# A spectral filter stage in a fused attention and long-convolution kernel: a ring block's matrix products issued one step after its VectorE work, and a mix with the projections by weights

## The chip, the cores and the metric

The kernel runs on one core of a Trainium2 chip. The core has five engines with a queue of instructions each: TensorE (PE, matmuls; PEld is its weight load), VectorE (DVE), ScalarE (ACT), GpSimd (POOL) and SyncE (SP, which here only issues DMAs). Each engine works its own list in order; semaphores hold an instruction back until what it reads is there or the buffer it writes is free. The metric is the device time of the whole program in microseconds (us), and less is better. The kernel before takes 1736.26 us, the median of three runs from 1733.69 to 1740.81.

## The reference, cut to what matters

Two layers of a backbone run over 1024 latent tokens and 256 context tokens of width 1024: a latent attention layer and a gated long convolution. The long convolution multiplies spectra, and the spectra of its filters depend on parameters alone, so the kernel can compute them at any time before layer 1. This is the part that the change touches:

```python
def hyena_filter_spectra(L, w_in, w_hid, b, freq, w_out):
    ...
    for k, w in enumerate((w_in, w_hid[0], w_hid[1])):
        hdn = jnp.sin(freq[k] * (hdn @ w.astype(f32) + b[k]))
    h = (hdn @ w_out.astype(f32)).reshape(L, HY_ORDER, 2, HY_WIDTH)
    ...
    h = h * jnp.exp(-t * deltas)[:, None, None, :]
    hf, hb = h[:, :, 0], h[:, :, 1]
    k_circ = jnp.concatenate([hf[:1] + hb[:1], hf[1:], jnp.zeros_like(hf[:1]), hb[:0:-1]], axis=0)
    return jnp.fft.rfft(k_circ, axis=0)
```

Beside it runs the input projection of layer 0, `t @ w_in` in `mla_mixer`, which gives the queries' and keys' latent vectors, the rotary key and the gate.

## The kernel before, in words

All matrix products run in a reduced precision format, on operands split in two: `split` (L95) makes a high part on ScalarE (`copy`, L96) and a low part on VectorE (subtract, L97), and `mm3` (L117) multiplies three of the four pairs (L119, L120, L121). So every operand that a matmul reads has passed through ScalarE and VectorE.

`layer0_in` (L462) runs three kinds of work together:

- **The filter stage**, the generator `filters` (L286). After a small network (`filter_mlp`) it goes through eight groups of 128 channels. For each group g there are eight position blocks j: a decay tile `dec` of 128 KB is loaded (L314, two buffers), four matmuls make `ph` (L318, L319, two banks), VectorE multiplies it by `dec` into `kk` (L321) and forms the sum `kp` and the difference `km` (L328, L329). Then `ring` (L222, L225, VectorE alone) folds the group's eight blocks into eight blocks `blk` of a transform. Each block goes through `forward`: its split into `bh` (ScalarE) and `bl` (VectorE), then the products with the transform's matrices `fm` into a bank `u` (9 matmuls, 12 for block 0, so 75 of them for a group). ScalarE copies `u` to `ko` (L340), and SyncE stores it to `kd` (L351).
- **The projections**, the generator `work`, 46 steps: gate tiles, the latent keys with their norms, the rotary key, the context stream. Its matmuls write the banks `pj` and read the tiles `pg` (activations, split once) and `w` (weights, loaded into `wr` and split as they are needed, three buffers). A step is mostly 12 such matmuls. After `work` comes `latent_q`, three tiles of queries with their norms and two more gate tiles.
- **The modulation vectors**, the generator `ada`: weights `aw` are loaded in 512 KB pieces and multiplied by one column into the bank `ad` (L128).

A yield of these generators is where the next one may put its instructions. In the kernel before, `filters` yields once for each j and once after each ring block, 128 times; nine of these are used up before the mixing loop, and the loop then takes one step of `work` for every two steps of `filters` (L621). The projections' 46 steps are so given out after some 92 of the 119 steps that are left.

The place in the program is not the order on the engines. A list scheduler takes the program's order as priority and writes a fixed list for each engine, taking a later instruction first where it reckons that the earlier one is not ready. The lists, not the yields, are what the chip runs. Below, *group g* is one of the eight channel groups, numbered from 0, *its first u* is the first matmul that writes `u` for it, and *round g* is the stretch from the first u of group g-1 to that of group g. *The last ring product* is the last matmul on `u` of group 7. What stands behind it up to the first attention score (`apx`) is called *the tail*.

Of the kernel before, what the change touches and what calls it, by code (L numbers as in the profile page):

```python
# [24 lines left out]
KD = D // P  # L25
# [30 lines left out]
class Net:  # L56
# [227 lines left out]
    def filters(self, psum, pt_h, pt_u, side):  # L284
# [15 lines left out]
        def load(g):  # L300
            wr = rp.tile([P, 512], F32, tag="fwr", name="fwr", bufs=1)
            wh, wl = [rp.tile([P, 512], F32R, tag=f"fw{r}", name="fw", bufs=1) for r in range(2)]
            nc.sync.dma_start(out=wr, in_=a["fwout"][g])
            self.split(wr, wh, wl)
            return wh, wl

        nxt = load(0)
        for g in range(KD):
            wh, wl = nxt
            kp = [gp.tile([P, 4, CS], F32, tag="rg", name=f"kp{i}") for i in range(2)]  # L310
            km = [gp.tile([P, 4, CS], F32, tag="rg", name=f"km{i}") for i in range(2)]
            for j in range(8):
                dec = rp.tile([P, 2, 1, P], F32, tag="dec", name="dec", bufs=2)
                nc.sync.dma_start(out=dec, in_=a["dec"][g, j])  # L314
                ps = psum.tile([P, 2, 2, P], F32, tag=pt_h, name="ph")
                ts = slice(P * j, P * j + P)
                for d, h in ((0, self.hf), (1, self.hr)):
                    nc.tensor.matmul(ps[:, d], lhsT=h[:, ts], rhs=wh[:, 256 * d : 256 * d + 256], start=True, stop=False)  # L318
                    nc.tensor.matmul(ps[:, d], lhsT=h[:, ts], rhs=wl[:, 256 * d : 256 * d + 256], start=False, stop=True)  # L319
                kk = rp.tile([P, 2, 2, P], F32, tag="kk", name="kk")  # L320
                nc.vector.tensor_tensor(out=kk, in0=ps, in1=dec.broadcast_to([P, 2, 2, P]), op=ALU.mult)  # L321
                if j == 0:
                    bias = rp.tile([1, 2, P], F32, tag="hb", name="hbias", bufs=1)
                    nc.sync.dma_start(out=bias, in_=a["hbias"][:, :, P * g : P * g + P])
                    nc.vector.tensor_tensor(out=kk[0:1, 0], in0=kk[0:1, 0], in1=bias, op=ALU.add)
                k0 = kp[j // 4][:, j % 4].rearrange("p (o c) -> p o c", o=2)
                k1 = km[j // 4][:, j % 4].rearrange("p (o c) -> p o c", o=2)
                nc.vector.tensor_tensor(out=k0, in0=kk[:, 0], in1=kk[:, 1], op=ALU.add)  # L328
                nc.vector.tensor_tensor(out=k1, in0=kk[:, 0], in1=kk[:, 1], op=ALU.subtract)  # L329
                if j == 0:  # L330
                    nc.vector.tensor_copy(out=km[0][0:1, 0], in_=kp[0][0:1, 0])
                yield
            if g + 1 < KD:
                nxt = load(g + 1)
            cl = slice((g % 2) * P, (g % 2) * P + P)

            def emit(i, b):
                u = self.forward(two, ubank, fm, i, b)
                ko = rp.tile([P, 2, CS], F32, tag="ko", name="ko")
                nc.scalar.activation(out=ko, in_=u, func=AF.Copy, scale=1.0 / 1024)  # L340
                r0 = 2 * i + 1
                if i == 0:
                    r0 = 0
                    kx = rp.tile([P, CS], F32, tag="kx", name="kx", bufs=1)
                    nc.vector.tensor_scalar(out=ko[0:1], in0=ko[0:1], scalar1=0.5, scalar2=None, op0=ALU.mult)
                    nc.scalar.copy(out=kx, in_=ko[:, 0])
                    nc.scalar.copy(out=kx[0:1], in_=ko[0:1, 1])
                    nc.vector.memset(ko[0:1, 1], 0.0)
                for o in range(2):
                    oc = slice(P * o, P * o + P)  # L350
                    nc.sync.dma_start(out=self.kd[o, g // 2, :, r0 : r0 + 2, cl], in_=ko[:, :, oc])  # L351
                    if i == 0:
                        nc.sync.dma_start(out=self.kd[o, g // 2, :, 2, cl], in_=kx[:, oc])

            for i, b in self.ring(two, lambda: gp.tile([P, 1024], F32, tag="rg", name="rg"), kp, km, False):
                emit(i, b)
                yield
        self.close("filtg", "filtr", "filt")


# [94 lines left out]
    def layer0_in(self):  # L455
# [16 lines left out]
        filt = self.filters(ps, "ph", "pu", "right")  # L472
# [144 lines left out]
                pass  # L617

        todo = work()
        n = 0  # L620
        for step, _ in enumerate(filt):  # L621
            while n * 120 < (step + 1) * 60:
                next(todo, None)
                n += 1
        for _ in todo:
# [822 lines left out]
```

## Time and profile before

| what | value |
| --- | --- |
| time, median of three runs | 1736.26 us |
| the profiled execution, its own time | 1731.71 us |
| span of its instructions | 1729.9 us |
| TensorE busy | 1633.5 us, 94% |
| VectorE busy | 1442.2 us, 83% |
| ScalarE busy | 766.3 us, 44% |
| mean granted TensorE clock | 0.979 |
| first `kk` and last `kk` of the filter stage | 26.9 and 376.4 us |
| first and last matmul on `u` of the stage | 59.8 and 403.3 us |
| first attention score (`apx`) | 439.8 us |

The profile takes one execution, 4.55 us shorter than the median of the three runs. "Busy" is the union of an engine's instructions; matmuls are pipelined and their modelled ends overlap the next one's start, so the start-to-start distance of matmuls in a dense run is the time that one takes, and not its listed duration. A wait is put down to the instruction or transfer that came last. Line numbers are those of the kernel before; the same functions stand up to ten lines further down after the change.

### The profile page before, as it was taken

Reading aid. Unit: us, or ns where it says so; the run is one execution under the profiler, and the core shown is the slowest. Engines: PE = TensorE matmul, PEld = TensorE weight load, DVE = VectorE, ACT = ScalarE, POOL = GpSimd, SP = SyncE. Lnnn points to the kernel's source line nnn. Section 1 sums busy time; section 2 is a strip of 40 time slices with the busy share of each in tenths; the row PEclk is TensorE's granted clock in tenths of the full one; section 3 lists DMA queues with packets and bytes.
Section 4 is the critical chain, followed back from the end, with each engine's and each line's share of the span. In section 5 each row is a group of like instructions: output and inputs, shape, how many; then the busy total and the mean of one; then the engine's idle time right before and its main releaser. Section 6 shows DMA issues by size and latency. Waiting matters only on the chain.

```text
span 1729.9 us, 22940 instructions
## 1 busy us (share of the span) xinstructions
PE 1633.5 (94%) x8160; PEld 1299.5 (75%) x8160; DVE 1442.2 (83%) x2558; ACT 766.3 (44%) x1337; POOL 16.0 (1%) x43
## 2 busy tenths in 40 slices
PE   5899897899999999999999999999999999999996
PEld 2467676787788788788787777888888888887874
DVE  4886979895699899899899456999999999999856
ACT  4533444445455465555555345433433433343313
POOL 1000000000000000000000010000000000000000
PEclk9899999899999999999999999999999999999998
DMA  9777664436101001010014771332332332244545
GB/s 342 256 231 222 200 187 120 138 89 206 28 27 37 25 32 38 19 33 25 25 56 132 232 254 64 101 98 83 101 115 83 104 106 89 95 122 134 180 142 197
DMA packets 140759, 206.15 MB, mean 119 GB/s; under 512 B 13578, under 2 KB 71649, under 8 KB 140516
## 3 DMA queue, kind: packets, MB, share of 16 engines
q1 hardware_dynamic: 137508, 194.00, 35.7%
q0 software_dynamic: 3136, 10.69, 1.9%
q8 instruction: 64, 1.05, 0.3%
q14 instruction: 51, 0.42, 0.1%
HBM read 148.92 MB, written 53.61 MB: 117 GB/s over the span
## 4 chain that ended last, share of the span: by engine, by line
PE 75%; DVE 10%; DMA 9%; ACT 3%; issue 2%; SPq 1%; DVEq 0%; ACTq 0%
PE pj L121 12%; PE pj L119 12%; PE pj L120 12%; DMA dec<-in_dec 2%; PE O L120 2%; PE S L119 2%; PE O L119 2%; PE S L826 2%; PE O L121 2%; PE apx L762 2%; PE S L825 2%; PE S L121 2%; PE S L120 2%; PE apx L763 2%; PE fu L119 2%; PE fy L119 2%
## 5 line engine op out<-in xcount | busy, mean ns | idle before, releaser
L96 ACT CAST w<-wr 128x512 fp32r<-128x512 f32 (+1 forms) x149 | 90.7, 609 | 259.5 <-PE pj L120 129.5
L119 PE MATMUL pj<-a,w 128*128 128x512 f32 x512 | 203.1, 397 | 1.7 <-ACT a L422 1.6
L121 PE MATMUL pj<-a,w 128*128 128x512 f32 x512 | 203.1, 398 | 0.0
L120 PE MATMUL pj<-a,w 128*128 128x512 f32 x512 | 203.0, 397 | 0.0
L828 ACT ACTIVATE p<-S 128x512 f32<-128x512 f32 x160 | 95.7, 598 | 148.2 <-DVE acc L835 69.5
L97 DVE TENSOR_TENSOR w<-wr,w 128x512 fp32r<-128x512 f32 (+1 forms) x149 | 98.8, 671 | 54.7 <-ACT w L96 54.6
L96 ACT CAST bh<-raw 128x512 fp32r<-128x512 f32 x128 | 77.1, 620 | 89.1 <-DVE raw L1071 71.0
L119 PEld LDWEIGHTS pj<-a,w 128*128 128x128 f32 x512 | 96.4, 188 | 22.0 <-ACT a L422 2.4
L120 PEld LDWEIGHTS pj<-a,w 128*128 128x128 f32 x512 | 96.5, 188 | 19.9 <-DVE a L423 0.2
L121 PEld LDWEIGHTS pj<-a,w 128*128 128x128 f32 x512 | 96.6, 189 | 19.5 <-issue 0.8
L97 DVE TENSOR_TENSOR p<-p 128x512 fp32r<-128x512 f32 x160 | 109.4, 684 | 1.5 <-ACT p L96 1.2
L764 DVE TENSOR_REDUCE cm<-apx 128x1 f32<-128x512 f32 (+1 forms) x192 | 107.1, 591 | 3.8 <-PE apx L763 3.1
L835 DVE TENSOR_TENSOR acc<-acc,p 128x512 f32<-128x512 f32 x144 | 98.7, 685 | 7.6 <-ACT p L828 6.7
L121 PE MATMUL pj<-pg,w 128*128 128x512 f32 (+1 forms) x248 | 96.5, 389 | 8.7 <-DVE w L97 8.6
L96 ACT CAST p<-p 128x512 fp32r<-128x512 f32 x160 | 99.5, 622 | 4.8
L119 PE MATMUL pj<-pg,w 128*128 128x512 f32 (+1 forms) x248 | 95.7, 389 | 2.7 <-ACT pg L422 2.7
L120 PE MATMUL pj<-pg,w 128*128 128x512 f32 (+1 forms) x248 | 96.6, 389 | 0.6 <-DVE pg L423 0.6
L97 DVE TENSOR_TENSOR bl<-raw,bh 128x512 fp32r<-128x512 f32 x128 | 84.7, 686 | 9.1 <-ACT bh L96 9.0
L119 PE MATMUL u<-bh,fm 128*128 128x256 f32 (+1 forms) x200 | 68.2, 342 | 12.2 <-ACT bh L96 9.5
L762 PE MATMUL apx<-kn,qn 128*128 128x512 f32 (+1 forms) x192 | 69.0, 364 | 2.2 <-DVE cm L764 1.9
L321 DVE TENSOR_TENSOR kk<-ph,dec 128x512 f32<-128x512 f32 x64 | 42.6, 684 | 33.2 <-DMA dec<-in_dec 26.6
L763 PE MATMUL apx<-krh,r 128*128 128x512 f32 (+1 forms) x192 | 67.1, 357 | 0.0
(312 smaller groups left out, 4408.9 us busy)
## 6 DMA issues: line engine op xcount, KB each, us to landing
aw<-in_adaw SPq DMA_DIRECT2D x32, 512.0 KB
kd<-ko SPq DMA_DIRECT2D x128, 128.0 KB
wr<-in_hw SPq DMA_DIRECT2D x64, 256.0 KB
kt<-kd SPq DMA_DIRECT2D x56, 256.0 KB
wr<-in_w SPq DMA_DIRECT2D x34, 256.0 KB
dec<-in_dec SPq DMA_DIRECT2D x64, 128.0 KB
pg<-in_adaw SPq DMA_DIRECT2D x32, 256.0 KB
wr<-in_wo SPq DMA_DIRECT2D x32, 256.0 KB
```

The source lines that it names most:

```text
L96: self.nc.scalar.copy(out=hi, in_=raw)
L97: self.nc.vector.tensor_tensor(out=lo, in0=raw, in1=hi, op=ALU.subtract)
L119: mm(out, lhsT=w[0], rhs=x[0], start=start, stop=False)
L120: mm(out, lhsT=w[0], rhs=x[1], start=False, stop=False)
L121: self.last = mm(out, lhsT=w[1], rhs=x[0], start=False, stop=stop)
L321: nc.vector.tensor_tensor(out=kk, in0=ps, in1=dec.broadcast_to([P, 2, 2, P]), op=ALU.mult)
L762: mm(b[:, :w], lhsT=qn[0][:, c], rhs=kn[0][:, o : o + w], start=True, stop=False)
L763: mm(b[:, :w], lhsT=r1[:, c], rhs=krh[:, o : o + w], start=False, stop=True)
L764: v.tensor_reduce(out=cm[:, t, i : i + 1], in_=b[:, :w], axis=AX.X, op=ALU.max)
L825: mm(S, lhsT=krh[:, c], rhs=r1, start=False, stop=False)
L828: act.activation(out=p, in_=S, func=AF.Exp, scale=ASCALE)
L835: v.tensor_tensor(out=acc, in0=acc, in1=p, op=ALU.add)
```

## The change

The step of `filters` now yields a weight: 3 for a position block j, 5 for each of three empty steps between the first ring block's VectorE work and anything else, and 4 for each ring block's products. The products of a block (with its split, its `ko` and its stores) are issued when the next block's ring work has been issued, and those of the last block at the end. A group weighs 3 x 8 + 5 x 3 + 4 x 8 = 71. The mixing loop gives out one step of `work` for every 8 x 67 / 50 = 10.72 of weight.

```diff
@@ -329,7 +329,7 @@
                 nc.vector.tensor_tensor(out=k1, in0=kk[:, 0], in1=kk[:, 1], op=ALU.subtract)
                 if j == 0:
                     nc.vector.tensor_copy(out=km[0][0:1, 0], in_=kp[0][0:1, 0])
-                yield
+                yield 3
             if g + 1 < KD:
                 nxt = load(g + 1)
             cl = slice((g % 2) * P, (g % 2) * P + P)
@@ -352,9 +352,17 @@
                     if i == 0:
                         nc.sync.dma_start(out=self.kd[o, g // 2, :, 2, cl], in_=kx[:, oc])
 
+            held = None
             for i, b in self.ring(two, lambda: gp.tile([P, 1024], F32, tag="rg", name="rg"), kp, km, False):
-                emit(i, b)
-                yield
+                if held is None:
+                    for _ in range(3):
+                        yield 5
+                else:
+                    emit(*held)
+                    yield 4
+                held = i, b
+            emit(*held)
+            yield 4
         self.close("filtg", "filtr", "filt")
 
 
@@ -617,9 +625,10 @@
                 pass
 
         todo = work()
-        n = 0
-        for step, _ in enumerate(filt):
-            while n * 120 < (step + 1) * 60:
+        n = passed = 0
+        for weight in filt:
+            passed += weight or 0
+            while n * KD * 67 < passed * 50:
                 next(todo, None)
                 n += 1
         for _ in todo:
```

No instruction is added or removed. What the lists of the engines make of it is seen at three places. In the rows, `ph` is the filter's product, `u` a ring product, `pj<-pg,w` a projection, `ad` and the `pj` with `ident`, `rms` or `st` are short pieces of the modulation and the norms.

**First, TensorE ahead of the first u of group 3.** Before, the row that starts group 4's `ph` is followed by a piece of a norm and 61 projection matmuls in a row, of which the first are shown:

```order
L319 MATMUL ph<-fw,hr 128x256
L318 MATMUL ph<-fw,hf 128x256
L414 MATMUL pj<-ident,rms 128x128 x4
L119 MATMUL pj<-pg,w 128x512
L120 MATMUL pj<-pg,w 128x512
L121 MATMUL pj<-pg,w 128x512
L119 MATMUL pj<-pg,w 128x512
```

Now the last `ph` of group 3, a piece of a norm, two blocks of group 4's `ph` and two steps of the modulation are all that stands there, and group 3's first u follows:

```order
L318 MATMUL ph<-fw,hr 128x256
L319 MATMUL ph<-fw,hr 128x256
L404 MATMUL pj<-ident,st 128x64 x4
L318 MATMUL ph<-fw,hf 128x256
L319 MATMUL ph<-fw,hf 128x256
L318 MATMUL ph<-fw,hr 128x256
L319 MATMUL ph<-fw,hr 128x256
L318 MATMUL ph<-fw,hf 128x256
L319 MATMUL ph<-fw,hf 128x256
L318 MATMUL ph<-fw,hr 128x256
L319 MATMUL ph<-fw,hr 128x256
L128 MATMUL ad<-aw,sc 32x512 x8
```

Round 3 held 61 projection matmuls and now holds 2.

**Second, VectorE at the first blocks of group 4.** Before, four instructions make two blocks, then come a piece of the context's modulation, the low parts of both blocks, and the next two blocks:

```order
L222 SCALAR_TENSOR_TENSOR rg<-rg 128x512 x2
L222 SCALAR_TENSOR_TENSOR blk<-rg 128x256 x4
L423 SCALAR_TENSOR_TENSOR pg<-pg,adac_87 128x256
L97 TENSOR_TENSOR bl<-blk,bh 128x512 x2
L222 SCALAR_TENSOR_TENSOR blk<-rg 128x256 x4
```

Now the order of the ring's own instructions is the same, with a piece of the later blocks' work where the modulation stood:

```order
L222 SCALAR_TENSOR_TENSOR rg<-rg 128x512 x2
L222 SCALAR_TENSOR_TENSOR blk<-rg 128x256 x4
L225 TENSOR_TENSOR rt<-rg 128x256
L97 TENSOR_TENSOR bl<-blk,bh 128x512 x2
L222 SCALAR_TENSOR_TENSOR blk<-rg 128x256 x4
```

Two blocks stand ahead of the first low part in both.

**Third, TensorE at the end of the stage.** Before, the last ring product is followed by the norm of the query tiles, after 647 + 13 of the 744 projection matmuls; 84 of them stand behind it:

```order
L121 MATMUL u<-bh,fm_104 128x256
L414 MATMUL pj<-ident,rms 128x128 x4
L128 MATMUL pj<-st,ones 32x512 x3
L119 MATMUL pj<-pg,w 128x512
L120 MATMUL pj<-pg,w 128x512
L121 MATMUL pj<-pg,w 128x512
L119 MATMUL pj<-pg,w 128x512
L396 MATMUL pj<-ident,st 128x96 x4
```

Now it is followed by 76 projection matmuls before those norms come, and 172 stand behind it:

```order
L119 MATMUL u<-bh,fm_103 128x256
L120 MATMUL u<-bl,fm_103 128x256
L121 MATMUL u<-bh,fm_104 128x256
L121 MATMUL pj<-pg,w 128x512
L119 MATMUL pj<-pg,w 128x512
L120 MATMUL pj<-pg,w 128x512
L121 MATMUL pj<-pg,w 128x512
L119 MATMUL pj<-pg,w 128x512
```

So 88 projection matmuls have moved from ahead of the last ring product to behind it.

## The prediction

> **What bounds the kernel now.** I read the page first, then the stretch of the filter stage cut at the first u of each group, then the waits of that stretch. The page gives the two engines that matter, and in its slices the stage lies in the first ten:
>
> ```profile
> span 1729.9 us, 22940 instructions
> PE 1633.5 (94%) x8160; PEld 1299.5 (75%) x8160; DVE 1442.2 (83%) x2558; ACT 766.3 (44%) x1337; POOL 16.0 (1%) x43
> PE   5899897899999999999999999999999999999996
> DVE  4886979895699899899899456999999999999856
> ```
>
> Over the whole span TensorE is the bound, so the end moves by what TensorE loses. It loses in slices 1 to 10, where VectorE is as full as it is. The cut by rounds (length; busy of PE, PEld, DVE, ACT, POOL; clock; DMA) shows which engine sets the pace of each; rows 1 to 7 are rounds 1 to 7, the eighth the ring products of group 7, the ninth the tail:
>
> ```profile
> 59.80:128.10 68.30, 62.39 (x337) 41.68 (x338) 56.82 (x119) 34.30 (x63) 0.00 (x0) 0.96 0.70 221
> 128.10:178.40 50.30, 47.95 (x264) 36.86 (x262) 33.32 (x70) 17.71 (x32) 0.00 (x0) 1.00 0.66 193
> 178.40:221.40 43.00, 36.96 (x199) 28.80 (x198) 39.03 (x88) 19.45 (x36) 0.00 (x0) 0.92 0.66 202
> 221.40:265.80 44.40, 39.75 (x222) 31.67 (x220) 35.02 (x74) 18.21 (x31) 0.00 (x0) 0.97 0.61 187
> 265.80:308.60 42.80, 29.53 (x183) 25.30 (x183) 39.36 (x83) 19.07 (x38) 0.00 (x0) 0.90 0.42 122
> 308.60:352.90 44.30, 43.85 (x217) 36.60 (x218) 36.07 (x81) 19.83 (x35) 0.00 (x0) 0.93 0.44 128
> 352.90:387.30 34.40, 34.01 (x185) 28.93 (x184) 31.23 (x64) 14.16 (x27) 0.00 (x0) 1.00 0.38 112
> 387.30:403.60 16.30, 16.30 (x100) 13.48 (x101) 12.73 (x29) 12.48 (x23) 0.00 (x0) 1.00 0.45 128
> 403.60:439.80 36.20, 32.24 (x145) 25.03 (x143) 14.62 (x28) 14.66 (x26) 3.70 (x7) 0.95 0.70 209
> ```
>
> Rounds 1, 2, 4, 6 and 7 are TensorE's. Rounds 3 and 5 are VectorE's: it is idle for 43.00 - 39.03 = 4.0 and 42.80 - 39.36 = 3.4 us, and TensorE waits. The longest of these waits is this one:
>
> ```profile
> 308.64 0.80 PE L119 MATMUL u<-bh,fm 128*128 128x512 f32 x1 [7.46 <-ACT bh L96]
> ```
>
> It is round 5's end. A group's first u must wait for its whole ring: in round 7, where no other work of VectorE lies between, the last two `kk` start at 375.84 and the first u at 387.26, so some 11 us after the group's last `ph` are VectorE's alone, and TensorE needs as much other work on its list there.
>
> ```profile
> 375.84 1.29 DVE L321 TENSOR_TENSOR kk<-ph,dec 128x512 f32<-128x512 f32 x2 [1.20 <-DMA dec<-in_dec]
> 387.26 0.49 PE L119 MATMUL u<-bh,fm 128*128 128x512 f32 x1 [0.39 <-ACT bh L96]
> ```
>
> **What TensorE's list is worth.** In dense stretches matmuls start this far apart:
>
> ```profile
> 318.09 0.28 PE L120 MATMUL u<-bl,fm 128*128 128x256 f32 x1
> 319.29 0.28 PE L121 MATMUL u<-bh,fm 128*128 128x256 f32 x1
> 322.14 0.39 PE L119 MATMUL pj<-pg,w 128*128 128x512 f32 x1
> 323.95 0.39 PE L121 MATMUL pj<-pg,w 128*128 128x512 f32 x1
> 115.48 1.07 PE L128 MATMUL ad<-aw,sc 128*32 128x512 f32 x8
> 319.71 0.38 PE L414 MATMUL pj<-ident,rms 128*128 128x128 f32 x2
> ```
>
> The first pair is 10 matmuls apart, 0.12 us each at 256 columns; the second 8 apart, 0.226 us each at 512. A modulation step takes about 1.0 us, a small transpose 0.15. Counting every matmul of each round in the lists at these prices gives, for rounds 1 to 7, the last ring products and the tail, in us:
>
> - before: 56.5, 45.8, 32.9, 37.8, 24.0, 39.5, 33.1, 15.5, 29.8;
> - now: 54.8, 45.6, 21.3, 43.7, 22.8, 23.0, 38.4, 13.5, 51.0.
>
> The measured lengths of before exceed the first line by 11.8, 4.5, 10.1, 6.6, 18.8, 4.8, 1.3, 0.8 and 6.4 us. These are the losses, 65 us in all. They are what the change can win, and the two lines say where it will not: between a group's last `ph` and its first u TensorE now has 3.6 us of work in round 3, 2.0 in round 5 and 1.0 in round 6, where the chain takes about 11. Before, only round 5 was so bare (4.4).
>
> **The change part by part.** *Products one step later.* This I cost at nothing: in the VectorE list two blocks stand ahead of the first low part in both kernels, so it is already in effect. Undone, it could cost one block's cast and subtraction per round (0.6 + 0.7 us from the groups below), not more; below nothing I exclude it, since the ring's order is the same.
>
> *Three empty steps and the weights.* They decide how much projection work lies in each round. No work is added, so the sum is that of the rounds. VectorE's part of each round I take from its busy time, corrected by what its list gains and loses, at these rows (all but the last from round 3, the last from round 5):
>
> ```profile
> L97 DVE TENSOR_TENSOR w<-wr,w 128x512 fp32r<-128x512 f32 x2 | 1.4, 684 | 0.0
> L97 DVE TENSOR_TENSOR pg<-pg 128x512 fp32r<-128x512 f32 x4 | 2.7, 688 | 1.4 <-ACT pg L96 1.4
> L523 DVE SCALAR_TENSOR_TENSOR pg<-pg,cols,pj 128x512 f32<-128x512 f32 x4 | 2.8, 746 | 1.3 <-PE pj L414 1.3
> L225 DVE TENSOR_TENSOR rt<-rg 128x256 f32<-128x256 f32 x1 | 0.4, 414 | 0.0
> L404 DVE TENSOR_TENSOR rms<-rms 128x4 f32<-128x4 f32 x2 | 0.3, 156 | 0.0
> L421 DVE SCALAR_TENSOR_TENSOR pg<-pg,gs,pj 128x256 f32<-128x256 f32 x7 | 2.9, 456 | 0.0
> ```
>
> - Round 3 loses four `pg` low parts (2.7), three L523 (2.1) and seven `rms` (1.1): 39.0 - 5.9 = 33.1.
> - Round 4 gains these 5.9 and two `rt` (0.8), loses two `w` (1.4), two context pieces (0.8) and four small additions (0.6): 35.0 + 3.9 = 38.9.
> - Round 5 loses three `w` (2.1) and two `rt`, gains one context piece and four small additions: 39.4 - 1.9 = 37.5.
> - Round 6 gains two `w`, loses three context pieces, one `pg`, two `rt` and five `rms`: 36.1 - 2.2 = 33.9.
> - Round 7 gains two `rt`, four context pieces, a `pg` and five `rms`: 31.2 + 4.0 = 35.2.
>
> VectorE's own waits are the unknown, since they depend on what each instruction now stands behind. Before they were, by the waits from 75 to 430 us:
>
> ```profile
> DVE kk L321 <- DMA dec<-in_dec: 16.7, 10, 5.2
> DVE w L97 <- ACT w L96: 12.8, 4, 7.7
> DVE bl L97 <- ACT bh L96: 8.4, 12, 2.3
> DVE kk L321 <- PE ph L319: 6.1, 4, 2.1
> ```
>
> The decay tiles have two buffers, so a load can only start when a `kk` is done; that stays, and SyncE's list still mixes them with the `ko` stores and the modulation's loads. In rounds 3 to 7 VectorE idled between 3.2 us (34.40 - 31.23) and 9.4 (44.40 - 35.02). In rounds 3, 5 and 6 of now TensorE's list is short, as in rounds 3 and 5 of before, so I take their mean, 3.7, and keep 0 and 8.2 (round 6) as ends.
>
> The sum: rounds 3, 5, 6 are VectorE's, 33.1, 37.5, 33.9 plus 3.7 each: 36.8, 41.2, 37.6. Rounds 4 and 7 are TensorE's, and follow a stall, as round 6 did before: its loss of 4.8 on 43.7 and 38.4 gives 48.5 and 43.2. Rounds 1 and 2 keep their losses: 66.6 and 50.1; the last products 14.3. So the last u comes 338.3 us after the first, where it was 343.8: 5.5 us sooner. But the tail grows from 29.8 to 51.0 us of matmuls, and there TensorE has nothing to overlap with but itself: with the loss of before 57.4. Sum 395.7 against 380.0: 15.7 us longer. The tail's rows of before confirm the count (28 of each line, 84) and show the largest piece of its loss, which I keep:
>
> ```profile
> L121 PE MATMUL pj<-pg,w 128*128 128x512 f32 x28 | 11.8, 420 | 3.5 <-DVE w L97 3.5
> 403.78 0.54 POOL L656 DMA_DIRECT2D ckv<-ckv_d  x1 [385.37 <-PE u L121]
> ```
>
> The loads on the GpSimd queue that wait for the last ring product have 51 us of cover where they had 30, so nothing is late there. After the tail the lists are those of before. On the profiled execution's 1731.71 us (span 1729.9 and 1.8 around it) this is 1747.4; the median of three was 4.55 above that execution, so I add the same 15.7 to 1736.26: 1752.0.
>
> **A price that the clock adds.** The stall before 308.64 was followed by a slow clock:
>
> ```profile
> 301.20:304.40 3.20, 0.00 (x0) 0.00 (x0) 3.20 (x6) 0.74 (x2) 0.00 (x0) 1.00 0.31 102
> 304.40:308.60 4.20, 0.00 (x0) 0.00 (x0) 4.20 (x10) 0.62 (x1) 0.00 (x0) 0.50 0.21 62
> 308.60:314.60 6.00, 5.96 (x20) 5.06 (x20) 6.00 (x17) 3.44 (x5) 0.00 (x0) 0.50 0.25 70
> ```
>
> The granted clock fell to 0.50 some 3.2 us into the stall and stayed for 6.0 us after it: 3.0 us of TensorE lost, inside the 4.8 of round 6. The Trainium skill ("TensorE: Matmul & The Clock Gate", "Part 1: The HAM clock gate") says that the clock halves after about one idle window of 3.4 us and is full again after about 3.4 us of work. The trace agrees on the start and not on the end: by the rule a stall would cost 1.7 us, and rounds 4 and 7 together 2.6 less.
>
> **The rivals.** *VectorE's waits shrink* (not slower): for 12.8 us it waited for a weight's cast, which waits for `w` buffers that TensorE frees late. With TensorE less loaded in rounds 3, 5 and 6 this may go, and 2.0 of waiting be left in each (35.1, 39.5, 35.9); rounds 4 and 7 then lose 1.3 as round 7 did (45.0, 39.7), and the tail's 3.5 goes as well (53.9). With 66.6, 50.1 and 14.3 the sum is 380.1: no change, 1736. Against it: `dec` and `bh`, four fifths of the other waits shown, do not hang on projections. *The mix does what it is written for* (faster): if VectorE never idles in rounds 3 to 7 and TensorE loses nothing there, they take 33.1, 43.7, 37.5, 33.9 and 38.4, and the tail 52.0: 369.6, 1726; it decides where the three waits of VectorE together fall below some 3 us. Against it: no round of before came below 3.2 alone. *The clock multiplies the stalls* (slower still): three stalls of some 12 us where one of 7.46 stood; if the slow first products delay `ko`, the next `ph` and so VectorE, 3.0 more in each of rounds 3, 5 and 6: 1761. *The change doesn't act*: the steps are in the program, but the lists' 61 against 2 projections in round 3 show that it acts, only not as cover.
>
> **How the numbers follow.** Chances: 0.60 for the sum (1744 to 1759), 0.20 for the shrunken waits (1735 to 1744), 0.13 for the clock, 0.07 for faster. The range of 8 in 10 takes in VectorE's waits at 8.2 in three rounds (1765) and most of the shrunken ones: 1738 to 1765. A measurement of this kernel can tell about 0.5%, 8.7 us, from no change: slower by more 0.68, within it 0.26 (the second case and the forecast's low edge), faster 0.06.
>
> **What would show it.** Right: rounds 3, 5 and 6 of 37 to 41 us with 12 to 18 us of TensorE idle each, ended by a wait of u for `bh`; the last u some 5 us sooner; a tail near 57 us that starts with projections without a gap. Wrong: a tail that VectorE stalls, rounds 3, 5 and 6 under 35 us, or first u times over 45 us apart in them.

## The result, and the profile after

The changed kernel takes 1753.07 us, the median of four runs from 1750.74 to 1755.58. The kernel before, run beside it, takes 1736.89 (1733.69 to 1740.81, four runs). The ratio is 1.0093, with an interval from 1.0075 to 1.0112: some 0.9% slower. The forecast was 1752.0, in a range from 1738 to 1765.

The profiled execution took 1750.74 us. The page after, its first part and the slices of the two engines:

```profile
span 1748.7 us, 22935 instructions
PE 1640.0 (94%) x8160; PEld 1301.0 (74%) x8160; DVE 1443.4 (83%) x2558; ACT 765.1 (44%) x1337; POOL 16.1 (1%) x43
PE   6899697798999999999999999999999999999996
DVE  4886979983499898899889556999999999999956
```

The work is the same. TensorE's row falls to 6 in slice 5 and to 7 in slice 8 (8 and 8 before), and VectorE's to 3 and 4 in slices 10 and 11 (5 and 6 before), where the longer tail now lies. From slice 12 on the rows are nearly those of before.

The cut by rounds, after (columns as in the prediction: start and end, length, busy of PE, PEld, DVE, ACT, POOL, clock, DMA share, GB/s; rounds 1 to 7, the last ring products, the tail, and the rest of the span):

```profile
61.00:124.70 63.70, 58.98 (x326) 41.26 (x326) 55.58 (x116) 32.77 (x61) 0.00 (x0) 0.97 0.72 229
124.70:175.50 50.80, 47.53 (x261) 36.74 (x260) 34.32 (x70) 16.78 (x30) 0.00 (x0) 1.00 0.66 200
175.50:212.50 37.00, 26.32 (x154) 17.63 (x154) 33.16 (x73) 15.47 (x28) 0.00 (x0) 0.83 0.58 175
212.50:263.00 50.50, 47.71 (x241) 38.78 (x241) 39.72 (x84) 20.02 (x36) 0.00 (x0) 0.92 0.62 188
263.00:301.60 38.60, 27.84 (x149) 22.94 (x148) 34.38 (x73) 13.79 (x27) 0.00 (x0) 0.84 0.43 127
301.60:342.30 40.70, 28.01 (x175) 23.79 (x174) 37.46 (x81) 18.34 (x37) 0.00 (x0) 0.84 0.41 117
342.30:384.90 42.60, 41.80 (x207) 34.71 (x208) 35.26 (x77) 18.44 (x33) 0.00 (x0) 0.94 0.42 126
384.90:400.10 15.20, 14.76 (x87) 12.36 (x87) 11.08 (x21) 7.89 (x15) 0.00 (x0) 1.00 0.43 119
400.10:460.80 60.70, 53.75 (x243) 42.23 (x241) 18.46 (x39) 23.79 (x42) 3.69 (x7) 0.94 0.47 143
460.80:1748.70 1287.90, 1254.18 (x6175) 1016.84 (x6174) 1109.90 (x1862) 572.65 (x992) 5.96 (x16) 0.99 0.29 93
```

The sum from the first u to the first attention score is 399.8 us, where it was 380.0. The rest takes 1287.9, where it was 1290.1 (1729.9 - 439.8), and the first u comes 1.2 later (61.0 against 59.8): 19.8 - 2.2 + 1.2 = 18.8, the growth of the span. So the time lies in the filter stage, as forecast.

Inside it, TensorE's idle time is length less PE busy. Of the 19.8 us, 16.1 are idle time (from 37.0 to 53.1) and 3.7 longer busy time. The idle time gathers in three *bare* rounds, 3, 5 and 6, with 10.7, 10.8 and 12.7 us, and in the tail with 7.0. Before there was one such round, the fifth, with 13.3, and round 6, which had 0.5, is the one that changed most. The last u of the stage comes 3.5 us sooner (400.1 against 403.6), but it has more behind it: the first attention score is 21.0 us later.

What ended the three bare rounds, from the timeline of TensorE after (start, duration, instruction, and in brackets its idle time before it and what ended it): round 3, round 5, round 6.

```profile
210.37 1.94 PE L128 MATMUL ad<-aw,sc 128*32 128x512 f32 x8 [4.90 <-DMA aw<-in_adaw]
212.47 0.80 PE L119 MATMUL u<-bh,fm 128*128 128x512 f32 x1 [0.17 <-ACT bh L96]
...
298.70 0.58 PE L120 MATMUL pj<-pg,w 128*128 128x256 f32 x1 [5.20 <-DVE pg L431]
300.97 0.58 PE L120 MATMUL pj<-pg,w 128*128 128x256 f32 x1 [1.26 <-DVE pg L431]
...
342.33 0.79 PE L119 MATMUL u<-bh,fm 128*128 128x512 f32 x1 [8.61 <-ACT bh L96]
```

Only round 6 ends on the ring's `bh`. In round 3 a piece of the modulation that waits for its weights stands last ahead of u, and u itself then waits 0.17 us more, so `bh` came as late. In round 5 it is a piece of the context that waits for VectorE, and u behind it does not wait at all; but ScalarE's cast of the group's first `bh` ran there from 300.55 to 301.17 us, only 0.4 us before u started at 301.56. So in all three rounds the ring's `bh` was ready no sooner than some 0.4 us before u.

The tail loses more than it did. Three views of after show why: TensorE's timeline, ScalarE's, and the SyncE queue with its waits (us in total, times, longest).

```profile
424.82 0.58 PE L404 MATMUL pj<-ident,st 96*128 96x96 f32 x2 [6.52 <-ACT st L399]
...
423.19 0.62 ACT L96 CAST w<-wr 128x512 fp32r<-128x512 f32 x1 [7.30 <-DMA wr<-in_w]
...
424.19 0.58 ACT L399 COPY st<-pj 96x512 f32<-96x512 f32 x1
...
417.23 0.35 SPq L674 DMA_DIRECT2D cos<-in_rope  x1
417.63 0.43 SPq L675 DMA_DIRECT2D sin<-in_rope  x1
418.10 0.43 SPq L112 DMA_DIRECT2D wr<-in_w  x1
...
SPq L674 <- DMA kd<-ko: 9.9, 2, 9.6
```

Read from the last line up: SyncE's queue stood 9.9 us (two waits, the longest 9.6) ahead of the attention's table `cos`, which waits until the filter stage's stores to `kd` have landed. The two tables, 512 KB each, are then issued, and only behind them a weight of the projections. ScalarE's list stands at that weight's cast until 423.19, with the copy for a norm behind it, and TensorE waits 6.5 us for the copy. Before, SyncE waited as long there, by its waits of that kernel, but no weight load stood behind the tables:

```profile
SPq L665 <- DMA kd<-ko: 10.9, 4, 5.2
```

### The profile page after: what moved, and what is told of

It reads as the page before. It is cut to its first block, busy times and chain, and to the rows that moved or that the text cites. A ratio compares the mean times of both kernels' runs of the same rounds, so it can differ in the third digit from the quotient of the medians.

```text
span 1748.7 us, 22935 instructions
## 1 busy us (share of the span) xinstructions
PE 1640.0 (94%) x8160; PEld 1301.0 (74%) x8160; DVE 1443.4 (83%) x2558; ACT 765.1 (44%) x1337; POOL 16.1 (1%) x43
## 4 chain that ended last, share of the span: by engine, by line
PE 77%; DMA 9%; DVE 8%; ACT 3%; issue 2%; SPq 1%; DVEq 0%; ACTq 0%
PE pj L119 12%; PE pj L121 12%; PE pj L120 12%; PE O L120 2%; PE S L119 2%; PE O L119 2%; PE S L835 2%; DMA dec<-in_dec 2%; PE O L121 2%; PE apx L771 2%; PE S L834 2%; PE S L120 2%; PE S L121 2%; PE apx L772 2%; DMA aw<-in_adaw 2%; PE fu L119 2%
## 5 line engine op out<-in xcount | busy, mean ns | idle before, releaser
L120 PEld LDWEIGHTS pj<-a,w 128*128 128x128 f32 x512 | 96.4, 188 | 19.8 <-DVE a L431 0.3
L119 PE MATMUL u<-bh,fm 128*128 128x256 f32 (+1 forms) x200 | 67.8, 340 | 11.2 <-ACT bh L96 10.2
L120 PE MATMUL u<-bl,fm 128*128 128x256 f32 (+1 forms) x200 | 66.5, 334 | 2.0 <-DVE bl L97 1.9
```

Source lines behind the costliest of these rows:

```text
L119: mm(out, lhsT=w[0], rhs=x[0], start=start, stop=False)
L120: mm(out, lhsT=w[0], rhs=x[1], start=False, stop=False)
```

## The experiments

All of them ask what in the change makes the stage longer, and what holds a bare round. Times are medians; ratios are to the kernel before, run on the same chip.

| kernel | time, us | ratio | interval |
| --- | --- | --- | --- |
| after | 1753.07 | 1.0093 | 1.0075 to 1.0112 |
| 1 products one step later alone | 1734.1 | 0.9976 | 0.9959 to 0.9993 |
| 2 all but that | 1751.5 | 1.0077 | 1.0052 to 1.0103 |
| 3 after, rate 60 for 50 | 1729.82 | 0.9956 | 0.9928 to 0.9983 |
| 4 after, rate 40 for 50 | 1748.0 | 1.0060 | 1.0039 to 1.0080 |
| 5 after, `km` on GpSimd | 1750.65 | 1.0079 | 1.0064 to 1.0094 |
| 6 after, extra matmuls in the bare rounds | 1753.69 | 1.0098 | 1.0083 to 1.0113 |
| 7 after, rate 70 for 50 | 1734.91 | 0.9995 | 0.9984 to 1.0007 |
| 8 before, rate 66 for 60, `km` on GpSimd | 1725.24 | 0.9946 | 0.9928 to 0.9965 |
| 9 after without sums and differences | 1740.22 | 1.0023 | 1.0009 to 1.0037 |
| 10 before, rate 66 for 60 | 1726.48 | 0.9946 | 0.9926 to 0.9967 |
| 11 after without the empty steps | 1754.08 | 1.0108 | 1.0080 to 1.0135 |
| 12 number 9 with the matmuls of 6 | 1739.33 | 1.0021 | 1.0006 to 1.0037 |

### 1. The products one step later, alone

The kernel before with `held` and nothing else: no empty steps, the old mix.

```diff
+            held = None
             for i, b in self.ring(...):
-                emit(i, b)
-                yield
+                if held is not None:
+                    emit(*held)
+                    yield
+                held = i, b
+            emit(*held)
+            yield
```

> The kernel before, with one part of the change alone: a ring block's products are issued after the next block's VectorE work; the old mix of one step of other work for two steps is kept. Theory A (the pace of the mix is the cause): the lists hardly differ from before, 59 projection matmuls in round 3 where there were 61 and 84 in the tail as before, so the time is that of before within 4 us, 1733 to 1741. Rival B (the later products are the cause: each block's low part and its products come later, and TensorE waits for them): at least half of the loss is there, 1745 or more.

Measured: 1734.1 us, 0.9976 [0.9959, 0.9993]. The delay costs nothing; if anything it gains a little (0.2%). It is not the cause.

### 2. All of the change but the delay

The weights, the rate and the three empty steps stay, the products are issued at once.

```diff
-            held = None
+            first = True
             for i, b in self.ring(...):
-                if held is None:
+                if first:
                     for _ in range(3):
                         yield 5
-                else:
-                    emit(*held)
-                    yield 4
-                held = i, b
-            emit(*held)
-            yield 4
+                first = False
+                emit(i, b)
+                yield 4
```

> The changed kernel without the delay: a block's products are issued at once again, the three empty steps and the weights stay. Theory A: 2 projection matmuls in round 3, 38 and 61 in rounds 5 and 6, 169 in the tail, nearly as after the change, so 1750 to 1756. Rival B: within 4 us of before, 1733 to 1741.

Measured: 1751.5 us, 1.0077 [1.0052, 1.0103], the loss of the whole change. Its cut by rounds has the three bare rounds and the long tail again:

```profile
172.80:209.80 37.00, 26.29 (x154) 17.57 (x154) 33.05 (x72) 15.51 (x29) 0.00 (x0) 0.84 0.59 175
260.80:298.50 37.70, 27.06 (x148) 22.27 (x147) 34.41 (x73) 13.56 (x27) 0.00 (x0) 0.84 0.43 130
298.50:341.30 42.80, 30.36 (x178) 26.27 (x178) 39.61 (x86) 19.31 (x39) 0.00 (x0) 0.78 0.42 120
398.40:458.50 60.10, 52.88 (x240) 41.54 (x238) 18.40 (x39) 22.95 (x41) 3.69 (x7) 0.94 0.46 145
```

So the cause is in the mix. What is left are its rate, its weights and its empty steps.

### 3. The changed kernel with one number put back

A group of the kernel before is 16 steps, so 8 of `work`. After, it is 71 x 50 / 536 = 6.6. With 60 for 50 it is 7.9.

```diff
-            while n * KD * 67 < passed * 50:
+            while n * KD * 67 < passed * 60:
```

> The changed kernel with one number changed: 60 in place of 50 in the mixing loop, so one step of other work for 8.93 of weight in place of 10.72; delay and empty steps stay. Theory A: the list has 68, 70 and 117 projection matmuls in rounds 3, 5 and 6 and 84 in the tail, as before the change; the time is that of before within 4 us, 1733 to 1741, and the tail from the last ring product to the first attention score is 36 us as before. Rival C (the empty steps themselves leave TensorE bare, whatever the pace): it stays at 1748 or more.

Measured: 1729.82 us, 0.9956 [0.9928, 0.9983], a little faster than expected and faster than before. Rounds 3 and 6 and the tail are back:

```profile
177.80:221.50 43.70, 40.21 (x214) 31.68 (x213) 38.68 (x87) 19.48 (x37) 0.00 (x0) 0.92 0.63 199
309.80:355.40 45.60, 45.28 (x227) 37.80 (x228) 35.80 (x80) 19.80 (x35) 0.00 (x0) 0.95 0.42 124
404.40:438.70 34.30, 31.99 (x145) 24.91 (x142) 14.67 (x28) 14.57 (x26) 3.69 (x7) 0.95 0.75 228
```

Round 6 idles 0.3 us where it idled 12.7, and the tail is 34.3 us where it was 60.7. Round 5 keeps 11.2 us of idle time, as it had 13.3 before. One number undoes the loss, with the delay, the weights and the empty steps in place. The rate is nearly that of the kernel before (7.9 and 8), so the 0.4% by which this kernel is faster than that one is not the rate's; half of it may be the delay's (experiment 1), and the rest was not followed up.

### 4. The rate lowered further

```diff
-            while n * KD * 67 < passed * 50:
+            while n * KD * 67 < passed * 40:
```

> The changed kernel with 40 in place of 50: one step of other work for 13.4 of weight. Theory A, by the same sum of rounds: 51, 0, 27 and 64 projection matmuls in rounds 3, 4, 6 and 7 and 284 in the tail, 76 us of matmuls there where the changed kernel has 51; rounds 3, 4, 6 and 7 are VectorE's, so the first is some 10 us above the changed kernel: 1758 to 1770. Rival D (the mix is only too slow at one place, round 3, which here has 51 projections): below 1750.

Measured: 1748.0 us, 1.0060 [1.0039, 1.0080]. This was a miss: it should have lost some 10 us more than the changed kernel, and it lost no more, rather less. Rounds 2, 4, 6 and 7, the tail and the sum over the nine stretches:

```profile
122.00:162.10 40.10, 37.80 (x215) 28.54 (x213) 31.89 (x68) 14.23 (x27) 0.00 (x0) 1.00 0.78 238
...
195.00:235.70 40.70, 28.23 (x147) 19.00 (x147) 33.93 (x76) 14.01 (x25) 0.00 (x0) 0.75 0.65 199
...
283.80:318.70 34.90, 24.23 (x138) 20.48 (x137) 31.74 (x66) 12.45 (x24) 0.00 (x0) 0.84 0.43 125
318.70:361.50 42.80, 29.54 (x169) 25.43 (x169) 37.84 (x79) 18.20 (x37) 0.00 (x0) 0.82 0.36 103
...
378.00:456.60 78.60, 77.43 (x356) 61.81 (x354) 21.45 (x43) 30.57 (x52) 3.69 (x7) 1.00 0.45 135
sum 397.60, PE 347.68 PEld 274.23 DVE 299.99 ACT 167.39 POOL 3.69; mean PE 38.63 PEld 30.47 DVE 33.33 ACT 18.60 POOL 0.41
```

The tail grew by 17.9 us, but round 2, which TensorE had filled, became shorter by 10.7, and there are still three bare rounds, now 4, 6 and 7, with 12.5, 10.7 and 13.3 us idle. The tail idles 1.2 us where it idled 7.0. By this reading, which rests on this one cut and was not tested by itself, work that leaves a round for the tail costs little as long as the round stays covered, since the one loses much of what the other gains; what is paid for is a round left bare, with 10 to 13 us of TensorE in each. How many rounds are bare is a matter of where the lists put the work, and does not follow the rate smoothly.

### 5. `km` on GpSimd, to take work from VectorE

The prediction said that VectorE's work sets rounds 3, 5 and 6. The difference (L329) on GpSimd should take 64 x 0.42 us from VectorE.

```diff
-                nc.vector.tensor_tensor(out=k1, in0=kk[:, 0], in1=kk[:, 1], op=ALU.subtract)
+                nc.gpsimd.tensor_tensor(out=k1, in0=kk[:, 0], in1=kk[:, 1], op=ALU.subtract)
```

> The changed kernel with the 64 subtractions that make km (0.42 us each on VectorE) on GpSimd, which is busy 1% of the span. The lists of rounds 3, 5 and 6 have 22.0, 24.5 and 23.8 us of matmuls, as in the changed kernel (21.3, 22.8, 23.0), and the tail 50.8 (51.0). Theory E (VectorE sets the length of rounds 3, 5 and 6, TensorE waits): each of them is some 3 us shorter, 34, 36 and 38 us, and the time 1741 to 1748. Rival F (the rounds are held by the loads of the decay tiles, with two buffers, whatever VectorE has to do): rounds 3, 5 and 6 stay within 1 us and the time at 1750 to 1756. If one subtraction takes GpSimd over 1.5 us, it lies in the way itself, and the rounds get longer.

Measured: 1750.65 us, 1.0079 [1.0064, 1.0094]. But it did not test the point, because VectorE's busy time hardly fell: over the nine stretches from 299.43 to 296.49 us, by the sums of the two kernels' cuts, after first:

```profile
sum 399.80, PE 346.70 PEld 270.44 DVE 299.43 ACT 167.29 POOL 3.69; mean PE 38.52 PEld 30.05 DVE 33.27 ACT 18.59 POOL 0.41
```

```profile
sum 398.90, PE 348.46 PEld 271.14 DVE 296.49 ACT 167.35 POOL 59.90; mean PE 38.72 PEld 30.13 DVE 32.94 ACT 18.59 POOL 6.66
```

Experiment 9 takes the work away instead of moving it.

### 6. A full clock in the bare rounds

In rounds 3, 5 and 6 the granted clock is 0.83 and 0.84. To see what that costs, 40 matmuls into a spare bank were put ahead of the ring in groups 3, 5 and 6. Nothing reads them.

```diff
+            if g in (3, 5, 6):
+                spare = ubank().rearrange("p a c -> p (a c)")
+                for n in range(40):
+                    nc.tensor.matmul(spare, lhsT=fm[0][:, 4 + n % 8, :], rhs=self.hf[:, 0:512], start=True, stop=True)
```

> The changed kernel with 40 extra matmuls of 512 columns (9.0 us) in each of groups 3, 5 and 6, between the group's last ph and its first u, into a spare bank that nothing reads. All else stands in the lists as in the changed kernel. Theory G (the half clock that follows the stalls costs time of its own: 51 us of it in rounds 3 to 7 of the changed kernel, of which 13 us in rounds 4 and 7, where TensorE is the bound): the clock stays full in these rounds, rounds 4 and 7 are 3 to 4 us and 2 us shorter, rounds 3, 5 and 6 not longer; the time 1743 to 1749. Rival H (the half clock is hidden behind VectorE): rounds within 1 us, 1750 to 1756; and if the extra matmuls come in the way, 1757 or more.

Measured: 1753.69 us, 1.0098 [1.0083, 1.0113]: nothing gained. Rounds 3, 5 and 6 of this kernel:

```profile
174.30:213.80 39.50, 34.60 (x186) 26.25 (x186) 32.45 (x71) 15.60 (x28) 0.00 (x0) 0.91 0.46 131
264.50:301.60 37.10, 33.42 (x184) 28.24 (x185) 32.40 (x69) 13.01 (x24) 0.00 (x0) 1.00 0.45 133
301.60:346.50 44.90, 38.88 (x223) 32.76 (x222) 40.05 (x86) 18.96 (x39) 0.00 (x0) 0.92 0.38 112
```

The clock rose to 0.91, 1.00 and 0.92, and the three lengths add up to 121.5 us where they were 116.3: two are 2.5 and 4.2 us longer and one 1.5 shorter, which neither theory had. Rounds 4 and 7, which theory G had 3 to 4 and 2 us shorter, took 50.7 and 41.7 us where they took 50.5 and 42.6. At the end of rounds 3 and 6 u still waits for `bh`, 1.0 and 3.0 us, with the clock up and 120 more matmuls done. So the slow clock is not what these rounds wait for at their end. The test is not clean: the spare bank is taken from u's own banks (`ubank`), and in round 3 the extra matmuls waited 3.9 us for ScalarE's copy `ko`. What they cost by being in the way may hide a small gain.

### 7. The rate raised further

```diff
-            while n * KD * 67 < passed * 50:
+            while n * KD * 67 < passed * 70:
```

> The changed kernel with 70 in place of 50 in the mixing loop. The lists have 46.4, 31.6, 37.3, 33.4 and 24.0 us of matmuls in rounds 3 to 7 and 22.6 in the tail: rounds 3 and 5 get what the tail loses. Theory A: below the kernel with 60 (1729.8) if the rounds are better filled: the sum of rounds goes from 382 to 377, so 1722 to 1730. Rival I (over 60 VectorE has no more room, since every projection brings a weight's low part with it): 1730 to 1738.

Measured: 1734.91 us, 0.9995 [0.9984, 1.0007]: no difference to before, and above what theory A expected; the time is in the range of rival I, whose reason was not tested. The tail is shorter still (23.5 us), but rounds 3 and 4 take 51.4 and 49.7, and round 4 idles 12.6 us, 8.2 of them in one wait of u for `bh`. In steps of `work` for a group it is 9.3; of the rates tried on the changed kernel, 7.9 is the best.

### 8. The best of both so far

The kernel before, with the mix at 66 for 60 (8.8 steps for a group, where it had 8) and `km` on GpSimd, as in experiment 5. The first of the two edits:

```diff
-            while n * 120 < (step + 1) * 60:
+            while n * 120 < (step + 1) * 66:
```

> The kernel before with two edits: km on GpSimd, as in the run with it on the changed kernel, and 66 steps of other work in place of 60 for 120. The lists have 42.7, 32.2, 31.9, 32.7 and 28.1 us of matmuls in rounds 3 to 7 and 27.6 in the tail, VectorE's rounds are some 3 us shorter. If theory E holds, the sum of rounds falls by 14 us: 1720 to 1728. If rival F holds: 1732 or more.

Measured: 1725.24 us, 0.9946 [0.9928, 0.9965]: faster than both kernels. Number 10 tells what GpSimd has in it.

### 9. The changed kernel with less for VectorE to do

This kernel leaves out the sums and differences of the filter halves, so its filters are other ones; only its time is of use.

```diff
-                kk = rp.tile([P, 2, 2, P], F32, tag="kk", name="kk")
-                nc.vector.tensor_tensor(out=kk, in0=ps, in1=dec.broadcast_to([P, 2, 2, P]), op=ALU.mult)
+                for d, k in ((0, k0), (1, k1)):
+                    nc.vector.tensor_tensor(out=k, in0=ps[:, d], in1=dec[:, d].broadcast_to([P, 2, P]), op=ALU.mult)
...
-                nc.vector.tensor_tensor(out=k0, in0=kk[:, 0], in1=kk[:, 1], op=ALU.add)
-                nc.vector.tensor_tensor(out=k1, in0=kk[:, 0], in1=kk[:, 1], op=ALU.subtract)
```

> The changed kernel with the sums and differences of the two filter halves left out: the product with the decay goes straight to kp and km in two instructions of 256 columns (0.84 us for a position block) in place of one of 512 and two of 256 (1.52 us). No other engine gets work. The lists of TensorE are nearly those of the changed kernel: 22.0, 42.0, 25.2, 23.8 and 38.4 us of matmuls in rounds 3 to 7, 51.0 in the tail. Theory E (rounds 3, 5 and 6 are VectorE's work plus some 3.7 us of its waits): VectorE's work in a round falls by 5 to 6 us, and so do these three rounds, from 37.0, 38.6 and 40.7 to 31, 33 and 36; rounds 4 and 7, TensorE's, fall by less than 3; the time 1734 to 1742. Rival F (the decay tiles' loads, with two buffers, or the chain of waits between ph, kk and the loads, set the rounds): they fall by less than 2 us each and the time is 1748 or more.

Measured: 1740.22 us, 1.0023 [1.0009, 1.0037]. The time is as expected by theory E, that VectorE sets the bare rounds, but the rounds are not: 33.8, 36.1 and 44.2 us where it had 31, 33 and 36. Their rows and the sum:

```profile
171.30:205.10 33.80, 26.74 (x151) 18.75 (x151) 28.16 (x64) 15.42 (x28) 0.00 (x0) 0.85 0.57 167
251.90:288.00 36.10, 27.57 (x163) 23.71 (x161) 27.60 (x60) 12.87 (x25) 0.00 (x0) 0.94 0.52 151
288.00:332.20 44.20, 32.24 (x182) 27.46 (x181) 35.58 (x80) 20.77 (x41) 0.00 (x0) 0.77 0.39 114
...
sum 391.40, PE 344.70 PEld 270.44 DVE 266.29 ACT 167.59 POOL 3.69; mean PE 38.30 PEld 30.05 DVE 29.59 ACT 18.62 POOL 0.41
```

VectorE does 33.1 us less in the nine stretches, and these are 8.4 us shorter: a quarter. Most of that was won in rounds 1, 2 and 4 (1.4, 1.8 and 3.7 us). By the medians it is a third (1753.07 - 1740.22 = 12.9 us, where the pages' VectorE rows differ by 1443.4 - 1405.1 = 38.3); the profiled execution of this kernel, 1744.51 us, is the slowest of its ten. In the three bare rounds it is busy 13.7 us less (from 105.0 to 91.3), and they are 2.2 us shorter (116.3 to 114.1); VectorE now idles in them 5.6, 8.5 and 8.6 us, where it idled 3.8, 4.2 and 3.2. It does hold the stage in part, but other things stand close behind it. VectorE's longest waits in these rounds are for a decay tile in round 3 (3.2 us), for ScalarE's cast of a weight in round 5 (3.8) and, in round 6, 2.0 each for the cast `bh` and for a projection of TensorE: no single one.

### 10. One number changed in the kernel before

The diff of experiment 8, without GpSimd.

> The kernel before with one number changed: 66 steps of other work for 120 in place of 60, VectorE's work as before. The lists have 39.7, 35.2, 32.8, 32.9 and 32.2 us of matmuls in rounds 3 to 7 (before 32.9, 37.8, 24.0, 39.5, 33.1) and 23.5 in the tail (29.8): more even than any other. Theory A (an even share of projections in the rounds is what counts): the sum of rounds is 6 us below before, 1728 to 1733. Rival (the gain of the run with km on GpSimd and 66 came from GpSimd): 1735 to 1740.

Measured: 1726.48 us, 0.9946 [0.9926, 0.9967]: as fast as number 8, so GpSimd gave nothing that can be seen. It is a little below what was expected, and with number 8 the fastest of all. Rounds 4 and 5, the tail and the sum over its nine stretches:

```profile
228.50:276.30 47.80, 39.67 (x220) 33.69 (x220) 40.44 (x89) 21.32 (x40) 0.00 (x0) 0.93 0.42 129
276.30:318.50 42.20, 38.17 (x201) 31.76 (x200) 36.79 (x81) 20.02 (x37) 0.00 (x0) 0.91 0.49 149
...
407.40:431.80 24.40, 23.98 (x113) 19.44 (x111) 11.40 (x19) 12.50 (x22) 3.69 (x7) 1.00 0.92 280
sum 371.60, PE 341.82 PEld 266.88 DVE 299.46 ACT 171.26 POOL 3.69; mean PE 37.98 PEld 29.65 DVE 33.27 ACT 19.03 POOL 0.41
```

No round is bare any more: the longest idle time is 8.1 us, in round 4, and round 5 has 4.0 where before had 13.3. TensorE idles 29.8 us in all, where it idled 37.0 before and 53.1 after.

### 11. The empty steps taken out, at the same rate

Without three steps of weight 5 a group weighs 56. With 64 for 50 it still gets 6.7 steps of `work`.

```diff
-                if held is None:
-                    for _ in range(3):
-                        yield 5
-                else:
+                if held is not None:
...
-            while n * KD * 67 < passed * 50:
+            while n * KD * 67 < passed * 64:
```

> The changed kernel without the three empty steps, with 64 in place of 50 in the mixing loop: a group then weighs 56, and 56 x 64 gives out the projections at nearly the rate of 71 x 50 (6.7 and 6.6 steps for a group). Theory A (the rate alone decides): the lists have 11, 39 and 64 projection matmuls in rounds 3, 5 and 6 and 169 in the tail, nearly those of the changed kernel, and the time is 1748 to 1755. Rival C (the empty steps put the loss where it is): below 1743.

Measured: 1754.08 us, 1.0108 [1.0080, 1.0135], the loss of the whole change. Rounds 3, 5 and 6 idle 10.3, 10.8 and 12.0 us, and the tail takes 61.0. The empty steps are not the cause: without them, at the same rate, the loss is the same.

### 12. Less for VectorE, and a full clock

Number 9 with the extra matmuls of number 6: when VectorE holds the rounds less, does the clock begin to count?

> The run without sums and differences with the 40 extra matmuls of the warm run in groups 3, 5 and 6. Without sums VectorE's work in rounds 3, 5 and 6 fell by 5.0, 6.8 and 1.9 us, and their lengths by 3.2 and 2.5, while the last grew by 3.5 with 20 us of half clock in it. Theory G, as left over (once VectorE is lighter, the half clock in which the ring products then run sets the pace): the clock stays full, round 6 falls from 44 to 38 us and the time to 1730 to 1736. Rival H (the clock is hidden here too, and the rounds are a chain through VectorE, ScalarE and the ring products that no one engine sets): 1738 to 1745.

Measured: 1739.33 us, 1.0021 [1.0006, 1.0037], the time of number 9. In the cut by rounds the clock is full in rounds 3, 5 and 6 (1.00, 1.00, 0.99), and TensorE's idle time over the nine stretches is 25.9 us, where number 9 has 46.7. The three rounds take 31.9, 35.9 and 43.3 us, 3.0 less than in number 9 together; theory G had 6 less in round 6 alone. By the medians 0.9 us is gained, which is within the scatter. At most a few us hang on the clock here.

## Why the prediction was right, point by point

**The sum.** The lists of TensorE, with the losses of the stage before and VectorE's work in three rounds, gave the stage its length: 395.7 us forecast, 399.8 measured. By rounds (forecast, measured): 66.6, 63.7; 50.1, 50.8; 36.8, 37.0; 48.5, 50.5; 41.2, 38.6; 37.6, 40.7; 43.2, 42.6; last products 14.3, 15.2; tail 57.4, 60.7. Round 1 lost 8.9 us where it had lost 11.8. That the last u comes 338.3 us after the first is as measured (339.1). The mechanism is as forecast; that the median came within 1.1 us (1753.07 for 1752.0) is in part luck. The errors of the nine stretches lie between -2.9 and +3.3 us and partly cancel, and the stage's growth of 19.8 us, 4.1 above the forecast, was made less by the rest of the span and by the scatter of single executions: the medians lie 16.2 us apart, the two profiled executions 19.0.

**The cause.** The prediction put it in the mix, which takes work from the rounds to the tail and leaves three rounds bare, and the runs bear this out: experiment 2 has the loss without the delay, 11 without the empty steps, and in 3 the loss is gone when only the rate is raised again. "Products one step later" at nothing was right (experiment 1).

**Mis-sized: the tail's loss.** It was kept at the 6.4 us of before, and was 60.7 - 51.0 = 9.7. That the two are so near is chance, since the pieces are others: the 3.5 us in which TensorE waited for a weight's low part are gone, and almost all of the tail's idle time of 7.0 us is now one wait, by TensorE's waits of after from 400 to 461 us:

```profile
PE pj L404 <- ACT st L399: 6.5, 1, 6.5
```

The prediction asked only the GpSimd queue whether anything came late. The late transfer was on SyncE's: a weight load behind two tables that wait for the filter's stores. In experiment 4, whose tail is longer, TensorE idled 1.2 us in it, so the loss does not follow the tail's length. No run moved the load alone; this is read from the trace.

**Rounds 3, 5 and 6.** Their lengths were right, and so were VectorE's waits in them (3.8, 4.2 and 3.2 us where 3.7 was taken). VectorE's work was 33.16, 34.38 and 37.46 us for 33.1, 37.5 and 33.9: some 3 us of round 5's work was done in round 6, and the two lengths are off by as much, in opposite directions. TensorE's idle time was forecast at 12 to 18 us each and was 10.7, 10.8 and 12.7, since TensorE ran slower in them and so was busy for longer. That the rounds end on u's wait for `bh` was right as it stands for round 6 alone; in rounds 3 and 5 another wait stood ahead of u, and `bh` was ready at about the same time.

**Rounds 4 and 7.** Each was given the 4.8 us that round 6 of before lost behind its stall; they lost 6.8 and 4.2. In round 7, behind the longest stall (8.61 us), the clock was 0.50 from 342.3 to 345 us, 0.67 on average in the next 3.0 us and full after that: some 4.7 us at half clock by this estimate, where before it was 6.0 behind a stall of 7.46.

**VectorE's work sets them.** Only partly shown. Experiment 9 took 33 us from VectorE in the stage and won 8.4 there. What else holds a bare round stays open. A chain from `ph` and the decay tile through `kk`, the ring and ScalarE's casts to u and back to the next `ph` is what remains to suspect; no experiment took it apart.

**The rivals.** VectorE's waits did not shrink to 2.0 us in the bare rounds (3.8, 4.2 and 3.2). By its waits of after from 75 to 430 us, the one for a weight's cast grew from 12.8 to 23.9 us:

```profile
DVE w L97 <- ACT w L96: 23.9, 8, 10.8
DVE kk L321 <- DMA dec<-in_dec: 18.7, 13, 7.3
```

But 20.0 of these 23.9 us lie in the tail, by its waits from 400.1 to 430 us:

```profile
DVE w L97 <- ACT w L96: 20.0, 4, 10.8
```

In rounds 3, 5 and 6 of after VectorE has no wait for a weight's cast. Before, it had 4.3 us of them in round 6 and none in rounds 3 and 5, so there was little to win. What is left in these rounds is above all the wait for decay tiles, 3.1, 2.8 and 1.3 us, which the prediction had named against this rival.

The clock did not multiply the stalls: the sum came out without it, and experiments 6 and 12 gave most of it back and gained nothing that the medians show. That the three waits fall away (faster) did not happen at 50; a mix that does come out faster than before gives out more work for each group than 50 does (7.9 in experiment 3, 8.8 in 8 and 10).

## What to carry to other kernels

Where two streams of work are mixed, count what each engine's list holds between the points at which it must wait, and look for the rounds that are left bare. Here the rate of the mix decided this, and where the steps are written mattered little once a scheduler had ordered the lists. A bare round here had 10 to 13 us of TensorE idle, and a step of the rate in either direction could leave another round bare (experiments 4 and 7). For each operand that work takes with it into a tail, look at what stands ahead of its load in the queue.

## What the runs showed of the hardware

**GpSimd beside VectorE.** With `km` on GpSimd (experiment 5), VectorE's `kp`, which has the same inputs and the same shape, became longer. The groups of VectorE from 75 to 400 us by tile (duration in ns, minimum, median, maximum), after and then experiment 5, with GpSimd's own:

```profile
L328 DVE TENSOR_TENSOR kp<-kk x54: 400/416/426, 102.4 to 375.1; 128x256 f32<-128x256 f32 x54
```

```profile
L328 DVE TENSOR_TENSOR kp<-kk x54: 349/552/964, 100.5 to 374.0; 128x256 f32<-128x256 f32 x54
...
L329 POOL TENSOR_TENSOR km<-kk x53: 727/917/2607, 101.6 to 374.1; 128x256 f32<-128x256 f32 x53
```

The median rose from 416 to 552 ns, the longest took 964, and the subtraction itself took 917 on GpSimd where it had taken 417 on VectorE. The 56 subtractions in the nine stretches took VectorE 23.1 us after the change, and without them it was only 2.9 us less busy. `kp` took 33.0 us there, 9.9 more than the 23.1 of after; the rest was not followed up. The Trainium skill ("SBUF — State Buffer", "SBUF: two separate sides") says that a VectorE instruction with two inputs in SBUF and a GpSimd instruction that reads SBUF hold a shared pair of ports in turn, each for its whole length. The longer `kp` agrees with this; no run here separates it from other causes.

**A full clock that gains next to nothing.** In experiment 12 TensorE's clock and idle time were restored in the bare rounds (0.85, 0.94 and 0.77 in number 9 became 1.00, 1.00 and 0.99), and the time stayed within the intervals: 1.0021 against 1.0023. In the two profiled executions the three rounds became 3.0 us shorter (from 114.1 to 111.1), with 120 more matmuls in them. The slow clock there was a mark of the stall and at most a small cost.
